# A decoder layer on one core: the output projection with tokens on the output's partitions, and expert loads of 2 MB from the fifth expert on

## Chip, core and metric

One core of one Trainium2 chip runs the whole program. The metric is the device time of one execution in microseconds (us). Engines: TensorE (PE in the rows, PEld its weight loads), VectorE (DVE), ScalarE (ACT), GpSimd (POOL) and SyncE (SP), whose queue issues nearly all loads from HBM.

## The reference, cut

The layer takes h (256 tokens by 1024 features) in float32. Sub-layer 1 mixes tokens by two branches (sparse attention and RWKV-7), gates and merges them and projects the result; sub-layer 2 sends each token to 2 of 32 experts of one group of eight.

```python
merged = jax.nn.sigmoid(gate_a) * (o_attn @ w_branch_attn[l]) + jax.nn.sigmoid(gate_r) * (o_rwkv @ w_branch_rwkv[l])
h = h + gt1 * (merged @ w_out[l])                 # w_out: 1024 x 1024
xn2 = _rmsnorm(h, moe_norm_g[l]) * (1.0 + sc2) + sh2
# routing: group = argmax of 4 group logits, then the top 2 of its 8 experts
hdn = jax.nn.silu(xt @ wg) * (xt @ wu)            # wg, wu: 1024 x 512, for each of 32 experts
acc + cw[:, None] * (hdn @ wd)                    # wd: 512 x 1024
h = h + gt2 * moe
```

## The kernel before

*Front.* Projections, RWKV, attention and gates are generators of work pieces, and the string ORDER says which generator goes next. LORD sorts the loads of weights, RESERVE keeps room for each stage. Float32 precision comes from `mm3` (L539 to 541): both operands are split in a high and a low part, and three matmuls stand for one. `split` (L526 to 529) makes the parts of a weight: a cast on ScalarE or GpSimd, a subtraction on VectorE or GpSimd, chosen by the two letters of SPLIT's entry for the stage. The last two pieces of the front are the branch projections "br" and "ba"; their merged output lies split in `xhi` and `xlo`, features on partitions.

*Output projection* (L1462 to 1527, "wo"). Eight blocks m of output features are on the partitions of PSUM and all 256 tokens in the columns. Weights come in four loads j of two k each (k: blocks of 128 input features). `out_part` takes the weights of block m at a stride, so that block m holds the features 8p+m:

```python
mm3(block(m), (w[0][:, m:1024:8], w[1][:, m:1024:8]), (mh[:, k, :], ml[:, k, :]), k == 0 and m > 5,
    k == 7 and m not in (0, 2, 4))
```

These are 8 m x 8 k x 3 = 192 matmuls. x was transposed into `h` (features on partitions) during the front (L1072). The residual is added by VectorE (L1519), squares and router logits follow by small matmuls (`squares`, L1485; `logits`, L1479), and `turn` (L1491) transposes h into `h2`, tokens on partitions.

*Routing* (L1562 to 1613) stands on VectorE for both halves of the tokens at once: the root of the mean square (L1562 to 1571), logits and top choices (L1578 to 1593). TensorE then makes the ranks (L1597), `places` one-hot tables, `begin` (L1714) copies h2 into the accumulators, and `fetch` (L1624) gathers the tokens of each expert: matmuls whose weights are h2 and whose moving operand is a one-hot table.

*Experts.* Four experts make a quad, eight quads in all; a quad's products are `row_in` and `rows_in` (L1645, L1639) for gate and up, L1666 for down. Each expert has 6 MB, the whole 201 MB. SyncE issues their loads in a fixed order (`pump`, L296), each into the first slot that is free: in the main arena, or in the two pools `sb1` and `sb2` that take the place of the split buffers after their last use. Quads 0 and 1 come in loads of 1 MB (quad 0's first gate in four row pieces of each expert), later ones in 2 MB (WHOLE = 2), the last quad's down weights in halves of 512 columns. The next quad's places, fetch and scatter stand between a quad's up and down products.

## Time and profile before

| | |
|---|---|
| device time, median of 3 runs | 801.64 us (800.87 to 804.71) |
| the profiled execution | 800.6 us, span 798.8 us |
| TensorE busy | 660.6 us, 83% of the span |
| VectorE, ScalarE, GpSimd busy | 277.0, 164.9, 132.9 us |
| moved by DMA | 261.36 MB, 327 GB/s in the mean |
| chain that ended last | DMA 33%, TensorE 27%, VectorE 1% of the span |

Times in the rows are microseconds from the start of the span. TensorE's granted clock is given as a share of full speed: 1.00 is 2.4 GHz, 0.50 is 1.2 GHz. Matmuls are pipelined, so a matmul's duration is longer than the distance from one start to the next; the distance is what a row of them costs.

### The profile page before, as it was taken

How to read it: one execution, taken by the hardware profiler on the slowest of the kernel's cores; microseconds unless marked ns; L12 is line 12 of the kernel's file. 1: busy time of each engine (PE TensorE's matmuls, PEld its weight loads, DVE VectorE, ACT ScalarE, POOL GpSimd, SP SyncE). 2: the span in 40 equal slices, each digit the busy share in tenths (PEclk: the TensorE clock that was granted, in tenths of full speed). 3: DMA queues.
4: the chain of work that ended last, by engine and by line, in shares of the span. 5: the costliest groups of instructions: out<-in, count | busy, mean ns of one | idle time of the engine just before them, and what ended most of it. 6: DMA issues, size and time to landing. Idle time of an engine off the chain costs nothing.

```text
span 798.8 us, 11321 instructions
## 1 busy us (share of the span) xinstructions
PE 660.6 (83%) x4657; PEld 379.2 (47%) x4657; DVE 277.0 (35%) x665; ACT 164.9 (21%) x350; POOL 132.9 (17%) x171
## 2 busy tenths in 40 slices
PE   5898988899999999989998586777676777778567
PEld 2785657568889889974442131131131132222112
DVE  2577799887255645141211061011010010010001
ACT  2445412343176631031110010010010010000000
POOL 1456643322235133220000000000000000000000
PEclk9899999999999999989999698889889899889879
DMA  9997476552758368249999999999999999999995
GB/s 334 392 309 245 143 261 241 175 192 81 244 191 284 106 235 344 66 162 377 422 420 428 427 425 431 425 427 432 425 428 429 427 427 428 427 428 427 427 394 201
DMA packets 53796, 261.36 MB, mean 327 GB/s; under 512 B 6864, under 2 KB 18128, under 8 KB 37360
## 3 DMA queue, kind: packets, MB, share of 16 engines
q1 hardware_dynamic: 53456, 260.11, 82.4%
q8 instruction: 37, 0.61, 0.3%
q10 hardware_dynamic: 288, 0.52, 0.2%
q14 instruction: 15, 0.12, 0.0%
HBM read 259.57 MB, written 1.05 MB: 326 GB/s over the span
## 4 chain that ended last, share of the span: by engine, by line
DMA 33%; PE 27%; DVE 1%; SPq 1%; POOL 1%; ACT 0%; issue 0%; ACTq 0%; POOLq 0%
DMA more<-in_expert_w_up_dram 12%; DMA more<-in_expert_w_down_dram 11%; DMA more<-in_expert_w_gate_dram 10%; PE ps_e L1639 10%; PE ps_e L1666 4%; PE ps_e L1624 2%; PE ps_a L541 1%; PE ps_a L539 1%; PE ps_a L540 1%; PE acc L1721 1%; PE ps_e L1673 1%; PE acc L1714 1%; SPq L296 1%; PE ps_r L539 0%; PE ps_r L540 0%; PE ps_r L541 0%
## 5 line engine op out<-in xcount | busy, mean ns | idle before, releaser
L1639 PE MATMUL ps_e<-arena,more 128*32 128x512 f32 x456 | 83.9, 693 | 24.2 <-DMA arena<-in_expert_w_gate_dram 18.3
L1639 PE MATMUL ps_e<-arena 128*32 128x512 f32 x424 | 81.9, 709 | 22.4 <-DMA arena<-in_expert_w_up_dram 12.4
L1666 PE MATMUL ps_e<-arena 128*32 128x512 f32 x360 | 73.5, 659 | 17.6 <-DMA arena<-in_expert_w_down_dram 12.9
L529 DVE TENSOR_TENSOR split<-arena,split 128x512 fp32r<-128x512 f32 x77 | 61.3, 805 | 57.7 <-POOL split L526 29.1
L528 ACT CAST split<-arena 128x512 fp32r<-128x512 f32 x71 | 43.3, 618 | 74.6 <-PE ps_g L540 29.3
L573 PE MATMUL ps_a<-split 128*128 128x256 f32 x360 | 52.1, 303 | 3.3 <-ACT split L484 1.9
L1650 ACT ACTIVATE arena<-ps_e 128x512 f32<-128x512 f32 x8 | 4.8, 597 | 239.2 <-PE ps_e L1639 239.2
L1651 DVE SCALAR_TENSOR_TENSOR arena<-arena,ps_e 128x512 f32<-128x512 f32 x8 | 5.5, 688 | 140.0 <-ACT arena L1650 140.0
L573 PEld LDWEIGHTS ps_a<-split 128*128 128x128 f32 x360 | 47.8, 204 | 12.6 <-issue 6.8
L529 POOL TENSOR_TENSOR split<-arena,split 128x512 fp32r<-128x512 f32 x33 | 45.3, 1372 | 48.6 <-ACT split L528 25.5
L1704 POOL TENSOR_TENSOR arena<-arena 128x256 f32<-128x256 f32 x8 | 4.9, 616 | 283.4 <-PE ps_e L1707 281.8
L1683 DVE TENSOR_TENSOR arena<-ps_e,more 128x512 f32<-128x512 f32 (+1 forms) x17 | 11.8, 692 | 112.9 <-PE ps_e L1666 103.7
L1639 PEld LDWEIGHTS ps_e<-arena,more 128*32 128x32 f32 x456 | 18.6, 126 | 60.8 <-issue 27.7
L1639 PEld LDWEIGHTS ps_e<-arena 128*32 128x32 f32 x424 | 18.2, 128 | 56.4 <-issue 26.1
L1666 PE MATMUL ps_e<-more,arena 128*32 128x512 f32 x88 | 34.9, 632 | 8.4 <-DMA more<-in_expert_w_down_dram 7.7
L526 POOL TENSOR_SCALAR split<-arena 128x512 fp32r<-128x512 f32 x39 | 26.8, 688 | 82.9 <-PE ps_r L540 23.8
L1639 PE MATMUL ps_e<-more,arena 128*32 128x512 f32 x56 | 31.3, 722 | 10.7 <-DMA more<-in_expert_w_gate_dram 10.7
L1666 PEld LDWEIGHTS ps_e<-arena 128*32 128x32 f32 x360 | 16.5, 117 | 49.0 <-issue 22.5
L1639 PE MATMUL ps_e<-more,more 128*32 128x512 f32 x56 | 30.3, 702 | 10.6 <-DMA more<-in_expert_w_up_dram 10.6
L1652 DVE SCALAR_TENSOR_TENSOR arena<-arena,ps_e 128x512 f32<-128x512 f32 x8 | 8.2, 1029 | 87.3 <-PE ps_e L1639 87.3
L539 PE MATMUL ps_g<-split 128*128 128x256 f32 x128 | 38.3, 299 | 0.0
L1624 PEld LDWEIGHTS ps_e<-arena,more 128*128 128x128 f32 x256 | 30.9, 196 | 12.9 <-issue 8.2
(379 smaller groups left out, 1263.0 us busy)
## 6 DMA issues: line engine op xcount, KB each, us to landing
arena<-in_expert_w_gate_dram SPq DMA_DIRECT2D x21, 2048.0 KB, 22.3
arena<-in_expert_w_up_dram SPq DMA_DIRECT2D x21, 2048.0 KB, 23.6
arena<-in_expert_w_down_dram SPq DMA_DIRECT2D x17, 2048.0 KB, 21.1
arena<-in_w_in_dram SPq DMA_DIRECT2D x18, 1024.0 KB, 8.1
arena<-in_expert_w_down_dram SPq DMA_DIRECT2D x18, 1024.0 KB, 17.9
arena<-in_ada_w_dram SPq DMA_DIRECT2D x16, 1024.0 KB, 6.8
arena<-in_expert_w_up_dram SPq DMA_DIRECT2D x14, 1024.0 KB, 9.8
arena<-in_expert_w_gate_dram SPq DMA_DIRECT2D x12, 1024.0 KB, 8.3
```

What stands on the lines that cost most here:

```text
L296: nc.sync.dma_start(out=dst, in_=src)
L526: nc.gpsimd.tensor_scalar(h, w, 1.0, 0.0, op0=OP.mult, op1=OP.add)
L528: nc.scalar.copy(h, w)
L529: (nc.gpsimd if p[1] == "P" else nc.vector).tensor_sub(l, w, h.bitcast(F32))
L539: nc.tensor.matmul(ps, l[0], r[0], start=start, stop=False)
L540: nc.tensor.matmul(ps, l[0], r[1], start=False, stop=False)
L573: nc.tensor.matmul(p, a[:, kk, :], b[:, 4 * hf + kk, :], start=(i == 0 and kk == KORD[0]), stop=(i == 2 and kk == KORD[-1]))
L1624: nc.tensor.matmul(ps[:, n * kk:n * kk + n], h2[:, a, 2 * k2 + kk, :], oh(a), start=(a == 0), stop=(a == 1))
L1639: nc.tensor.matmul(ps[32 * g:32 * g + 32, :], xg[:, k, 32 * g:32 * g + 32], w[:, k - 4 * i, :], start=(k == 0), stop=(k == 7))
L1652: nc.vector.scalar_tensor_tensor(hidb[0:r].rearrange("p (j q) -> p q j", j=4), thb[0:r].rearrange("p (q j) -> p q j", j=4), 0.5, psu[0:r, ...
L1666: nc.tensor.matmul(pss[c][32 * g:32 * g + 32, :], hTb[:, j, 32 * g:32 * g + 32], w[:, j - 2 * i, 512 * c:512 * c + 512], start=(j == 0), s ...
L1683: nc.vector.tensor_mul(Yb[0:r, c:c + 512], ps[0:r], gt2[0][0:r, g:g + 512])
```

## The change

The output projection has four blocks (a, c) in PSUM: half a of the tokens on the partitions, 512 output features c in the columns. The weights of its matmuls are now the split activations `xhi` and `xlo` (128 tokens, contiguous), the moving operand is 512 contiguous columns of w_out: 4 blocks x 8 k x 3 = 96 matmuls. The residual stream `h2` has tokens on partitions and features in natural order from the start; the transposes of x in the front, the zero matmuls ahead of the projection and the copies to h2 are gone, and `fetch` reads h2 as weights at a stride of 8. gt1 is spread over all partitions by `mod_bcast` (two matmuls). Squares are summed by ScalarE's accumulator, the transposes that the logits need are four matmuls for each block, and root and routing are done for each half of the tokens. The string LAST sets the order of the last k pair: O is a block's product, T its transposes, L its logits, N the root, R the routing.

`xhi` and `xlo` of the first four k lie in a pool of their own, so that `sb1` (now 4096 columns) is opened after the second weight load and `sb2` (6144) after the last block. Loads are 2 MB from quad 1 on (WHOLE = 1), and the last quad's up weights are halves too. `begin` goes block by block, two ahead of the row products and two between them; the weights of the routing (`weights`) are worked out after quad 0's first products; quad 1's preparation stands behind quad 0's down products. ORDER and LORD are other strings (not shown).

```diff
-RESERVE = (29696, 17408, 24576, 4096, 0)
+RESERVE = (25600, 17408, 20480, 4096, 0)
...
-SPLIT = (('PD', 'PD', 'AP', 'AD'), ('PD', 'PD', 'AP', 'AD'), ('PP', 'PP', 'AD', 'AD'), ('AD', 'AP', 'AD', 'AD'), ('AD', 'PD', 'AP', 'PD'))
+SPLIT = (('PD', 'PD', 'AP', 'AD'), ('PD', 'PD', 'AD', 'AD'), ('AP', 'PP', 'AP', 'AD'), ('AD', 'AP', 'AP', 'AD'), ('AD', 'PD', 'AP', 'PD'))
...
-WHOLE = 2
+WHOLE = 1
+BEGIN = 1
+LAST = 'O00 O01 O10 O11 O20 O21 T00 O30 T01 L00 O31 L01 N0 R0 T10 T11 N1 L10 L11'
...
-    B = Arena(fr.__enter__().tile([128, nB], F32R, name="split"), nB)
+    B = Arena(fr.__enter__().tile([128, nB - 2048], F32R, name="split"), nB - 2048)
+    fr1 = tc.tile_pool(name="fr1", bufs=1, side="right")
+    B1 = Arena(fr1.__enter__().tile([128, 2048], F32R, name="split1"), 2048)
...
-        return q >= WHOLE and not (n == "ed" and q == QUADS - 1)
+        return q >= WHOLE and not (n != "eg" and q == QUADS - 1)
...
-    nc.sync.dma_start(out=wrt[:, :, 0:4], in_=I["router_group_w"][0].rearrange("(p k) n -> p k n", p=128))
-    nc.sync.dma_start(out=wrt[:, :, 4:36], in_=I["router_expert_w"][0].rearrange("(p k) n -> p k n", p=128))
+    nc.sync.dma_start(out=wrt[:, :, 0:4], in_=I["router_group_w"][0].rearrange("(k p) n -> p k n", p=128))
+    nc.sync.dma_start(out=wrt[:, :, 4:36], in_=I["router_expert_w"][0].rearrange("(k p) n -> p k n", p=128))
...
-    xhi = B.get(8, T)
-    xlo = B.get(8, T)
+
+    xhl = [b.get(4, 2, T) for b in (B1, B)]
+
+    def xhi(k, s=slice(0, T)):
+        return xhl[k // 4][:, k % 4, 0, s]
+
+    def xlo(k, s=slice(0, T)):
+        return xhl[k // 4][:, k % 4, 1, s]
...
-        h = M(8, T)
...
+        h2 = M(2, D)
...
-        xt = M(2, D)
-        nc.sync.dma_start(out=xt, in_=I["x"][0].rearrange("(a p) d -> p a d", p=128))
...
+        nc.sync.dma_start(out=h2, in_=I["x"][0].rearrange("(a p) d -> p a d", p=128))
...
-        for q in range(4):
-            ps = PS()
-            for kk in range(2):
-                for a in range(2):
-                    nc.tensor.transpose(ps[:, kk * 256 + a * 128:kk * 256 + a * 128 + 128],
-                                        xt[:, a, 2 * q + kk:D:8], ident)
-            nc.scalar.copy(h[:, 2 * q:2 * q + 2, :], ps.rearrange(v2, a=2))
-            yield 0.5
-        A.free(xt)
...
-            gt1, sh2 = mod_cols(row1, (0, 2))
-            nc.vector.tensor_scalar(gt1, gt1, 0.5, None, op0=OP.mult)
+            gt1 = M(1024)
+            mod_bcast(gt1, row1, 0, 0.5)
+            sh2, = mod_cols(row1, (2,))
...
-    fr2.__exit__(None, None, None)
-    state["more"].append(Arena(pool(name="sb1", bufs=1, side="right").tile([128, nB2], F32, name="more0"), nB2))
...
-    psl = PS("r")
-    pso = [PS(t) for t in "aaarr"]
-
-    for ps in pso[0:3] + [psl]:
-        nc.tensor.matmul(ps, zero.bitcast(BF16), trib[:, None, 128:256].to_broadcast([128, 4, 128]), start=True, stop=False)
...
-    def logits(m):
...
-            nc.tensor.matmul(psl[:, 64 * a:64 * a + 36], h[:, m, 128 * a:128 * a + 128], wrt[:, m, :],
...
-    def turn(m):
-
-        pst = PS("g")
-        for a in range(2):
-            nc.tensor.transpose(pst[:, 128 * a:128 * a + 128], h[:, m, 128 * a:128 * a + 128], ident)
-        nc.scalar.copy(h2[:, :, m, :], pst[:, 0:256].rearrange("p (a c) -> p a c", a=2))
-
-    def block(m):
-        return pso[m // 2][:, 256 * (m % 2):256 * (m % 2) + 256] if m < 6 else pso[m - 3][:, 0:256]
-
-    def out_part(m, k, w):
-        mm3(block(m), (w[0][:, m:1024:8], w[1][:, m:1024:8]), (mh[:, k, :], ml[:, k, :]), k == 0 and m > 5,
-            k == 7 and m not in (0, 2, 4))
+    pso = [PS(t) for t in "aaar"]
+    psl = [PS("r"), PS("r")]
+    tb = [M(512), M(512)]
+    st = M(4)
+    hts = [hx[:, 512 * i:512 * i + 512].rearrange("p (k t) -> p k t", k=4) for i in range(2)]
...
+    def leave_room(name, cols, *before, **k):
+        for p in before:
+            p.__exit__(None, None, None)
+        state["more"].append(Arena(pool(name=name, bufs=1, **k).tile([128, cols], F32, name="more" + name), cols))
+        pump()
+
+    def out_part(a, c, k, w):
+        s = slice(128 * a, 128 * a + 128)
+        mm3(pso[2 * a + c], (xhi(k, s), xlo(k, s)), (w[0][:, 512 * c:512 * c + 512], w[1][:, 512 * c:512 * c + 512]), k == 0,
+            k == 7)
+
+    def residual(a, c):
+
+        hv = h2[:, a, 512 * c:512 * c + 512]
+        for o in (0, 256) if a and c else (0,):
+            r = slice(o, o + 256 if a and c else 512)
+            nc.vector.tensor_mul(tb[c][:, r], pso[2 * a + c][:, r], gt1[:, 512 * c:512 * c + 512][:, r])
+            (nc.vector if a else nc.gpsimd).tensor_add(hv[:, r], hv[:, r], tb[c][:, r])
+        nc.scalar.activation(tb[c], hv, AF.Square, scale=1.0 / 32, accum_out=st[:, 2 * c + a:2 * c + a + 1])
+
+    def turn(a, c):
+
+        ps = PS("g")
+        for kk in range(4):
+            nc.tensor.transpose(ps[:, 128 * kk:128 * kk + 128], h2[:, a, 512 * c + 128 * kk:512 * c + 128 * kk + 128], ident)
+        nc.scalar.copy(hts[c], ps.rearrange("p (k t) -> p k t", k=4))
+
+    def logits(a, c):
+
+        for kk in range(4):
+            k = 4 * c + kk
+            nc.tensor.matmul(psl[a][:, 0:36], hts[c][:, kk, :], wrt[:, k, :], start=(k == 0), stop=(k == 7))
...
-            if j < 3:
-                for m in range(8):
-                    out_part(m, 2 * j + kk, ws[kk])
-                continue
-            for m in range(8 if kk else 0):
-                for k2 in range(2):
-                    out_part(m, 6 + k2, ws[k2])
-                for n in {3: (0,), 4: (1,), 5: (2,), 6: (3,), 7: (4, 5)}.get(m, ()):
-                    logits(n)
...
-                    nc.vector.scalar_tensor_tensor(h[:, n, :], block(n), gt1[:, n:n + 1], h[:, n, :], op0=OP.mult, op1=OP.add)
...
-        done(("wo", j))
-
-    fr.__exit__(None, None, None)
-    state["more"].append(Arena(pool(name="sb2", bufs=1).tile([128, nB], F32, name="more"), nB))
-    h2 = state["more"][-1].get(2048, from_top=False).rearrange("p (a k c) -> p a k c", a=2, k=8)
-    turn(0)
-    turn(1)
-    logits(6)
-    turn(2)
...
-    squares()
-    for m in range(3, 8):
-        turn(m)
-    A.free(h)
-    A.free(gt1)
+            if kk:
+                done(("wo", j))
+            for n in range(4 if j < 3 else 0):
+                out_part(n // 2, n % 2, 2 * j + kk, ws[kk])
+        if j == 1:
+            leave_room("sb1", nB2 + 2048, fr2, fr1, side="right")
+    last[0] = None
+
+    def out_last(n, kk):
+        after_last(lambda: out_part(n // 2, n % 2, 6 + kk, ws[kk]))
+        if kk:
+            residual(n // 2, n % 2)
...
+    def root(a):
+
+        z, y, u = zz[:, :, a:a + 1], y8[:, a:a + 1], u8[:, a:a + 1]
+        nc.vector.scalar_tensor_tensor(z[:, 0], st[:, a:a + 1], 1e-6, st[:, 2 + a:3 + a], op0=OP.add, op1=OP.add)
+        nc.vector.tensor_scalar(y.bitcast(I32), z[:, 0].bitcast(I32), -0.5, float(0x5F3759DF), op0=OP.mult, op1=OP.add)
+        for r in range(1, 3):
+            nc.vector.tensor_scalar(z[:, r], z[:, 0], 0.25 ** r, None, op0=OP.mult)
+        for r in range(3):
+            nc.vector.scalar_tensor_tensor(u, y, y, z[:, r], op0=OP.mult, op1=OP.mult)
+            nc.vector.scalar_tensor_tensor(y, u, -3.0, y, op0=OP.add, op1=OP.mult)
+        nc.vector.tensor_scalar(rs2[:, a:a + 1], y, -0.125, None, op0=OP.mult)
...
+    def route(a):
...
+        nc.vector.tensor_scalar(selb[:, a], eq[:, a], -2.0e38, None, op0=OP.is_lt)
+
+
+    for what in LAST.split():
+        f, i = what[0], [int(c) for c in what[1:]]
+        if f == "O":
+            out_last(*i)
+        elif f in "TL":
+            after_last(lambda: (turn if f == "T" else logits)(*i))
+            if f == "L" and i[1]:
+                nc.scalar.copy(lg[:, i[0]], psl[i[0]][:, 0:36])
+        elif f == "N":
+            root(*i)
+        else:
+            route(*i)
+    leave_room("sb2", nB - 2048, fr)
...
+    acc = [acp.tile([128, 512], F32, name=f"acc{i}") for i in range(4)]
+
+    def begin(n):
+
+        nc.tensor.matmul(acc[n], ident, h2[:, n // 2, 512 * (n % 2):512 * (n % 2) + 512], start=True, stop=False)
+
+    for n in range(BEGIN):
+        after_last(lambda: begin(n))
+    route(1)
...
+            nc.tensor.matmul(psk[:, 32 * a:32 * a + 32], trib[:, 0:128], selb[:, a], start=True, stop=(a == 0))
+        nc.tensor.matmul(psk[:, 32:64], trib[:, 128:256], selb[:, 0], start=False, stop=True)
+
+    after_last(ranks)
+    for n in range(BEGIN, 2):
+        after_last(lambda: begin(n))
+    nc.vector.tensor_mul(rk, psk[:, 0:64].rearrange("p (a n) -> p a n", a=2), selb)
+
+    def weights():
+
+        nc.gpsimd.tensor_copy(sel, selb)
...
-                    nc.tensor.matmul(ps[:, n * kk:n * kk + n], h2[:, a, 2 * k2 + kk, :], oh(a), start=(a == 0),
+                    nc.tensor.matmul(ps[:, n * kk:n * kk + n], h2[:, a, 2 * k2 + kk:D:8], oh(a), start=(a == 0),
...
-    def begin():
-
-        for a in range(2):
-            for c in range(2):
-                nc.tensor.matmul(acc[2 * a + c].rearrange("p (c k) -> p c k", k=8), ident,
-                                 h2[:, a, :, 64 * c:64 * c + 64].rearrange("p k c -> p c k"), start=True, stop=False)
...
-                        fetch(0, [k2])
-                        for k in () if i else (2 * k2, 2 * k2 + 1):
-                            row_in(ps, XGb[0], need(("row", k)), k)
-                            done(("row", k))
+                        after_last(lambda: fetch(0, [k2]))
+                    for k in range(0 if i else 4):
+                        after_last(lambda: row_in(ps, XGb[0], need(("row", k)), k))
+                        done(("row", k))
+                        if k % 2:
+                            after_last(lambda: begin(2 + k // 2))
                     if i == 0:
                         continue
-                rows_in(ps, XGb[q % 2], [need((n, e, i)) for e in es], i)
+                    weights()
+                after_last(lambda: rows_in(ps, XGb[q % 2], [need((n, e, i)) for e in es], i), q == 0)
...
-            begin()
...
-        places(q + 1)
-        fetch(q + 1)
-        scatter(q + 1)
+
+        def prepare():
+            places(q + 1)
+            fetch(q + 1)
+            scatter(q + 1)
+
+        if q:
+            prepare()
...
+        if q == 0:
+            prepare()
```

TensorE from the last block to the ranks or accumulators. L539 to L541 (L550 to L552 after) are the projection's matmuls, L1479 and L1505 logits, L1491 and L1498 transposes, L1485 squares, L1597 ranks, L1592 `begin`. Before:

```order
L539 MATMUL ps_r<-split 128x256
L540 MATMUL ps_r<-split 128x256
L541 MATMUL ps_r<-split 128x256
L1479 MATMUL ps_r<-arena 128x36 x4
L1491 MATMUL ps_g<-arena 128x128 x4
L1479 MATMUL ps_r<-arena 128x36 x4
L1491 MATMUL ps_g<-arena 128x128 x2
L1485 MATMUL ps_r<-arena 128x1 x6
L1491 MATMUL ps_g<-arena 128x128 x10
L1597 LDWEIGHTS arena
L1597 MATMUL ps_g<-arena 128x32
L1597 LDWEIGHTS arena
```

After:

```order
L550 MATMUL ps_r<-split 128x512
L551 MATMUL ps_r<-split 128x512
L552 MATMUL ps_r<-split 128x512
L1498 MATMUL ps_g<-arena 128x128 x4
L1505 MATMUL ps_r<-arena 128x36 x4
L550 MATMUL ps_r<-split 128x512
L551 MATMUL ps_r<-split 128x512
L552 MATMUL ps_r<-split 128x512
L1505 MATMUL ps_r<-arena 128x36 x4
L1498 MATMUL ps_g<-arena 128x128 x8
L1505 MATMUL ps_r<-arena 128x36 x8
L1592 MATMUL acc_3227<-arena 128x512
```

Transposes and logits of half 0 now stand around the last matmuls, those of half 1 behind them; the squares are gone from TensorE.

VectorE from the last residual on. L1519, L1522 (L1490, L1491 after) are residuals and a square, L1562 to L1571 (L1544 to L1551) the root, L1578 to L1593 (L1555 to L1565) the routing. Before:

```order
L1519 SCALAR_TENSOR_TENSOR arena<-ps_r,arena 128x256 x2
L1522 TENSOR_TENSOR arena<-arena 128x256
L1562 TENSOR_SCALAR arena<-ps_r 128x2
L1563 TENSOR_SCALAR arena<-arena 128x2
L1565 TENSOR_SCALAR arena<-arena 128x2 x2
L1568 SCALAR_TENSOR_TENSOR arena<-arena 128x1 x2
L1571 SCALAR_TENSOR_TENSOR arena<-arena 128x1 x2
L1568 SCALAR_TENSOR_TENSOR arena<-arena 128x1 x2
L1571 SCALAR_TENSOR_TENSOR arena<-arena 128x1 x2
L1568 SCALAR_TENSOR_TENSOR arena<-arena 128x1 x2
L1571 SCALAR_TENSOR_TENSOR arena<-arena 128x1 x2
L1578 SCALAR_TENSOR_TENSOR arena<-ps_r,arena 128x36 x2
```

After, from half 1's last residual on:

```order
L1490 TENSOR_TENSOR arena<-ps_r,arena 128x256 x2
L1491 TENSOR_TENSOR arena<-arena 128x256 x2
L1551 TENSOR_SCALAR arena<-arena 128x1
L1555 SCALAR_TENSOR_TENSOR arena<-arena 128x36
L1557 TENSOR_REDUCE arena<-arena 128x1
L1558 MATCH_REPLACE arena<-arena 128x8
L1561 SCALAR_TENSOR_TENSOR arena<-arena 128x32
L1544 SCALAR_TENSOR_TENSOR arena<-arena 128x1
L1562 MAX arena<-arena 128x8
L1545 TENSOR_SCALAR arena<-arena 128x1
L1547 TENSOR_SCALAR arena<-arena 128x1
L1563 COPY arena<-arena 128x2
```

The root of half 0 now stands ahead of these rows; its routing and half 1's root alternate.

SyncE's loads at the turn from quad 0 to quad 1: `arena`, `more` and `moresb` are where a load goes, 128x2048 is 1 MB, 128x4096 2 MB. Before:

```order
L296 DMA arena<-in_expert_w_down_dram 128x2048 x2
L296 DMA more<-in_expert_w_down_dram 128x2048
L296 DMA arena<-in_expert_w_down_dram 128x2048
L296 DMA more<-in_expert_w_down_dram 128x2048 x2
L296 DMA arena<-in_expert_w_down_dram 128x2048 x2
L296 DMA arena<-in_expert_w_gate_dram 128x2048 x8
L296 DMA arena<-in_expert_w_up_dram 128x2048 x7
L296 DMA more<-in_expert_w_up_dram 128x2048
L296 DMA more<-in_expert_w_down_dram 128x2048 x2
```

After:

```order
L300 DMA moresb_3057<-in_expert_w_up_dram 128x2048
L300 DMA moresb_3057<-in_expert_w_down_dram 128x2048
L300 DMA arena<-in_expert_w_down_dram 128x2048 x2
L300 DMA moresb_3216<-in_expert_w_down_dram 128x2048 x3
L300 DMA arena<-in_expert_w_down_dram 128x2048 x2
L300 DMA arena<-in_expert_w_gate_dram 128x4096 x4
L300 DMA arena<-in_expert_w_up_dram 128x4096
L300 DMA moresb_3057<-in_expert_w_up_dram 128x4096
L300 DMA arena<-in_expert_w_up_dram 128x4096
L300 DMA moresb_3216<-in_expert_w_up_dram 128x4096
```

Three of quad 0's last six loads go to the second pool, and quad 1 begins with loads of 2 MB.

## Rows read from the trace of the kernel before

**Rows 1.** Slices of the page: GB/s that DMA moved, 40 slices of 20 us.

```profile
GB/s 334 392 309 245 143 261 241 175 192 81 244 191 284 106 235 344 66 162 377 422 420 428 427 425 431 425 427 432 425 428 429 427 427 428 427 428 427 427 394 201
```

**Rows 2.** Windows, TensorE: stretch, length, busy (instructions), granted clock, DMA share, GB/s.

```profile
0.00:300.30 300.30, 272.79 (x2477) 0.97 0.66 229
...
306.00:337.00 31.00, 31.00 (x131) 1.00 0.48 177
...
356.70:363.00 6.30, 5.80 (x19) 0.57 0.99 416
```

**Rows 3.** Timeline, SyncE's loads: start, duration, queue, line, operation, destination and source, count.

```profile
325.78 11.87 SPq L296 DMA_DIRECT2D arena<-in_expert_w_down_dram  x2
348.85 0.33 SPq L296 DMA_DIRECT2D more<-in_expert_w_down_dram  x1
...
367.64 7.36 SPq L296 DMA_DIRECT2D arena<-in_expert_w_gate_dram  x6
```

**Rows 4.** Timeline, TensorE, projection's end to experts; [idle before, its releaser].

```profile
348.42 0.40 PE L541 MATMUL ps_r<-split 128*128 128x256 f32 x1
348.66 0.98 PE L1479 MATMUL ps_r<-arena 128*128 128x36 f32 x8
...
356.67 0.23 PE L1597 MATMUL ps_g<-arena 128*128 128x32 bf16 x2 [2.18 <-DVE arena L1593]
...
357.43 2.05 PE L1714 MATMUL acc<-more,arena 128*128 128x512 f32 x2 [0.50 <-DVE arena L1608]
359.30 1.89 PE L1624 MATMUL ps_e<-arena,more 128*128 128x128 f32 x8
...
362.82 1.50 PE L1645 MATMUL ps_e<-arena 128*32 128x512 f32 x12
```

**Rows 5.** Timeline, TensorE: branch projections, then the output projection's first matmul.

```profile
299.64 0.28 PE L539 MATMUL ps_g<-split,split 128*128 128x256 f32 x1
299.76 0.28 PE L540 MATMUL ps_g<-split,split 128*128 128x256 f32 x1
...
300.30 0.51 PE L539 MATMUL ps_a<-split 128*128 128x256 f32 x1
```

**Rows 6.** Timeline, TensorE: query projection.

```profile
162.24 0.40 PE L541 MATMUL ps_a<-split 128*128 128x512 f32 x1
162.48 0.39 PE L539 MATMUL ps_a<-split 128*128 128x512 f32 x1
```

**Rows 7.** Timeline, splits of weights in the output projection.

```profile
317.99 0.62 ACT L528 CAST split<-arena 128x512 fp32r<-128x512 f32 x1 [5.14 <-PE ps_r L540]
317.99 0.62 POOL L526 TENSOR_SCALAR split<-arena 128x512 fp32r<-128x512 f32 x1 [5.15 <-PE ps_r L540]
...
318.64 0.69 DVE L529 TENSOR_TENSOR split<-arena,split 128x512 fp32r<-128x512 f32 x1 [4.47 <-POOL split L526]
318.69 1.78 POOL L529 TENSOR_TENSOR split<-arena,split 128x512 fp32r<-128x512 f32 x1
```

**Rows 8.** Timeline, VectorE: a residual, start of root, start of routing.

```profile
348.86 0.48 DVE L1519 SCALAR_TENSOR_TENSOR arena<-ps_r,arena 128x256 f32<-128x256 f32 x1 [1.41 <-PE ps_r L541]
...
352.44 0.16 DVE L1562 TENSOR_SCALAR arena<-ps_r 128x2 f32<-128x2 f32 x1 [2.56 <-PE ps_r L1485]
...
354.22 0.41 DVE L1578 SCALAR_TENSOR_TENSOR arena<-ps_r,arena 128x36 f32<-128x36 f32 x2
```

**Rows 9.** Windows, all engines: PE, PEld, DVE, ACT, POOL; clock, DMA, GB/s.

```profile
370.00:380.00 10.00, 10.00 (x96) 2.86 (x88) 0.69 (x1) 1.16 (x3) 0.00 (x0) 1.00 1.00 407
...
400.00:420.00 20.00, 20.00 (x140) 8.53 (x136) 3.02 (x8) 2.47 (x6) 0.62 (x1) 1.00 1.01 421
500.00:600.00 100.00, 71.78 (x408) 23.57 (x406) 9.81 (x21) 5.53 (x13) 1.23 (x2) 0.86 1.01 428
```

**Rows 10.** Timeline, TensorE: a fetch, and quad 1's first expert matmuls.

```profile
385.52 3.73 PE L1624 MATMUL ps_e<-arena,more 128*128 128x128 f32 x32
...
397.80 7.89 PE L1639 MATMUL ps_e<-arena,more 128*32 128x512 f32 x66
```

More of the change, by code (lines that the diff above doesn't have):

```diff
@@ new lines, in layer_kernel @@
+    for what in LAST.split():
[11 more added lines that the diff above has]
+    leave_room("sb2", nB - 2048, fr)
+    A.free(gt1, *tb)
+    pump()
+    pctx.__exit__(None, None, None)
```

158 lines of the change are left out of this document (58 added, 100 removed).

## The prediction

> **What bounds the kernel now.** I read the page's slices first (20 us each, counted from 0): from slice 19 to the last but two DMA moves 420 to 432 GB/s, in slice 16 it moves 66 and in 17 it moves 162 [rows 1]. So the second half is a stream of expert weights (32 x 6 MB = 201 MB) at a constant rate, and the end is the time at which this stream gets going, plus bytes by rate. In the first half TensorE is the busy engine: 272.8 of the first 300.3 us [rows 2]. Between the two the stream starves, because SBUF is full and slots are freed only by the output projection, the routing and the first experts. SyncE's timeline shows that: two loads from 325.8, one at 348.9, the first loads of quad 1 from 367.6 [rows 3]. The reader is to see what each of them follows on TensorE: 348.9 the last projection matmul of 348.42, 367.6 the first expert products from 362.82 [rows 4]. An earlier start of the experts is therefore worth its full length, as long as the stream doesn't run dry later.
>
> **The projection.** Call s the start of its first matmul, 300.30 [rows 5]. Before: 192 matmuls of 256 columns, the last from 348.42 to the logits' start at 348.66 [rows 4]: 48.4 us, 0.25 a matmul, 0.24 the last. The same shape (128x128 weights, 256 columns) starts every 0.12 us in the branch projections just ahead [rows 5]. It is not the clock: in 306 to 337 the granted clock is 1.00 [rows 2], the 2.4 GHz level. The one difference in the code is that the weights are read at a stride of 8 elements. After: 96 matmuls of 512 columns with 128 contiguous columns as weights; that form stands in the query projection and starts every 0.24 us [rows 6]. 96 x 0.24 = 23.0. Among the last blocks now stand 8 transposes and 4 matmuls for logits. Eight 128x128 fp32 matmuls took 1.89 us in 359.3 to 361.2 [rows 4], where the clock was 0.57 [rows 2]; at the full level I take half, 0.9. Four logit matmuls are half of 0.98 [rows 4], 0.5. The logits wait for ScalarE's copy of the transposes, which stands behind squares: 1.0, somewhat more than one 512-column operation there (0.62 [rows 7]); and 0.2 for the last k's start. The last projection matmul ends at s+25.6, where it was s+48.4: 22.8 less.
>
> **Splits.** Each k needs two splits, a cast (0.62 on ScalarE or GpSimd) and a subtraction (0.69 on VectorE, 1.78 on GpSimd [rows 7]). A k now lasts 12 x 0.24 = 2.9 on TensorE instead of 5.8 or more. By SPLIT's last row ('AD', 'PD', 'AP', 'PD') two k cost GpSimd two casts and a subtraction, 2 x 0.62 + 1.78 = 3.0, VectorE 3 x 0.69 = 2.1, ScalarE 1.2, against 5.8 on TensorE. If the engines run side by side that is enough, and I cost it at nothing; as one chain, 0.62 + 1.78 + 0.62 + 0.69 = 3.7, it would not be (rival 1).
>
> **From the last projection matmul to the first expert.** Before, 14.2 us: logits, squares and turns until VectorE's root at 352.44, the routing of both halves from 354.22, ranks at 356.67, two pairs of matmuls that start the accumulators (the first pair 2.05) with fetch between, experts at 362.82 [rows 4, 8]. After, half 0's residual, squares and root lie beside the last blocks, and its routing stands between the steps of half 1's root on VectorE. Half 1 keeps its residual in two pieces of 256 columns, four operations of 0.48 [rows 8], 1.9; the square and two handovers, 0.9 (0.62 as above and 0.3); the root, 1.7 (352.44 to 354.22 is 1.8 for both halves [rows 8], and one half has the same chain of dependent steps); the routing, 1.8 (354.22 to 356.67 is 2.4 for both). Half 1's turn and logits hide beside the root. That is s+31.9. Then ranks, product and places, 1.8 (ranks to fetch was 2.6 [rows 4], with an accumulator pair ahead of the fetch), and fetch with its copies 2.5. Fetch has got slower work: it takes h2 in natural order as weights, at a stride of 8 elements, as the old projection did. I price its 8 matmuls like those, 8 x 0.24 = 1.9 (contiguous they took 1.89 at the low clock [rows 4] and 3.73 for 32, 0.12 each, at the full one [rows 10]), and 0.6 for copies. First expert matmul at s+36.2, bounds 35.3 (the stride costs fetch nothing) and 38 (all at 1.2 GHz, where the strided fetch may take 3.7). The gain is 62.5 - 36.2 = **26.3**, 22.8 of it in the projection, the rest in the gap of 10.6 after 14.2.
>
> **What is late next: the stream.** Call the first expert matmul R before and R' after. Before, quad 1's first load is issued at R+4.8 [rows 3, 4], with some of quad 0 still queued, whose last I put at R+8 (two loads of 1 MB, 2.5 us each at 421 GB/s [rows 9], ahead of it). After, by the order of the loads, three of quad 0's are let go by the last projection matmul and two by the first row products; the latter two land at about R'+7.8 by the same count. The first 2 MB load follows the last of the row products; the second follows the first half of the gate, a hole that I put at 0.5. Net +0.3.
>
> **2 MB loads.** In quad 1 the 1 MB loads ran at 407 and 421 GB/s, the 2 MB loads later at 428 [rows 9]: 25 MB, 62 us at 407 and 59 at 428, a gain between 0 and 3 (62 - 59); the 407 holds for 10 us only, so I take 0.5 (10 us by 5% of 407 against 428). The price is that a slot of 2 MB comes free later. Eight such loads last 8 x 4.9 = 39 us, so the stream runs dry at R'+47 unless a ninth is issued. The ninth waits until quad 1's gate has been read. Before, quad 1's first matmul is at 397.80, R+35.0, and half of that group's 7.89 us [rows 10] makes it R+39. After, TensorE has more to do until there: quad 1's fetch, 32 matmuls at 0.24 instead of 0.12, 3.9; the rest of quad 0's fetch, half as much, 1.9; against that one of the two accumulator pairs now lies ahead of R', 2.0 less. R'+43: a cover of 4 us. In later quads fetch's 3.9 is hidden, as TensorE is busy for 72 of 100 us in 500 to 600 [rows 9]; without that cover it would be 3.9 for each of some six quads, 23.
>
> **Ahead of the projection.** Gone are 16 transposes, 2 x 0.9 = 1.9, and four zero matmuls of 512 columns, 4 x 0.24 = 1.0. New are two fp32 matmuls that spread gt1 over the partitions, between 1.0 and 2.05 (a pair took 2.05 near the low level [rows 4]); I take 1.9. Net -1.0. The planner's tables (ORDER, LORD, SPLIT, RESERVE) are new too and rearrange 300 us in which TensorE idles 27.5 [rows 2]; no row prices that. I take 0, with -4 and +4 as bounds, a seventh of that idle time either way. The tail does the same work; its loads in halves: 0.
>
> **Sum.** -26.3 + 0.3 - 0.5 - 1.0 = -27.5. The profiled execution took 800.6, which gives 773.1; it lies 1.0 under the median of 801.64, by which it is 774.1. I say **773.5**.
>
> **Rivals.**
> 1. *Splits bound the projection.* If each k pays the whole chain, 3.7 and 0.4 of handovers instead of 2.9, six k add 7: 780. For: GpSimd's 1.78 alone is more than half of a k's 2.9 [rows 7]. Against: two pairs of buffers, and 3.0 of 5.8 on the busiest engine. 0.08.
> 2. *The queue runs dry between quads 0 and 1.* It decides from 4 us of lateness of quad 1's gate beyond my count, which a strided fp32 fetch at 0.36 or more a matmul would bring; a hole of 3 to 8 gives 777 to 781. For: preparing quad 1 now stands behind quad 0's down products, with the slower fetch. Against: the count. 0.09.
> 3. *The front's new order gives back* what the removed work saves, with 4 to 6 us of new waits: 779. For: 27.5 us of idle time that hang on the order. 0.04.
> 4. *Matmul time follows columns, however weights lie.* The projection then keeps its 48 us (192 x 256 columns are 96 x 512), and only the gap's 3.6 and the 1.2 of the other terms remain: 796. Against: 0.12 and 0.24 for one shape at one clock [rows 2, 4, 5]. 0.02. The Trainium skill has this rule ("TensorE: Matmul & The Clock Gate", section "Back-to-back issue gap"): 262 cycles for 256 columns, 518 for 512, and no term for the layout of the weights. The branch rows agree with it, the old projection's rows do not.
> 5. *Slower than before: TensorE stays at the 1.2 GHz level through quads 0 and 1*, because the gap breaks up its work, as at 356.7 to 363.0, where 0.57 was granted [rows 2]. Each quad could then take up to its 35 us more; the queue empties from 4 us of lateness, each further one is one at the end, and from 4 + 28 = 32 on the kernel is slower than before: 802 to 812. Against: clock 1.00 from 370 on [rows 9]. 0.03.
>
> **How the numbers follow.** Forecast 0.74, rivals 0.26. The forecast's own range is -4 and +4 for the front, -0.9 and +1.8 for the gap, -0.5 and +0.5 for the rate: 768 to 780. To hold 8 in 10 it takes in rivals 1 to 3 above, and below the whole 3 of the rate: **765 to 782**. Faster by over 0.5% (about what a measurement of this kernel can tell from no change; below 797.6) are the forecast and rivals 1 to 3: 0.74 + 0.08 + 0.09 + 0.04 = 0.95. Rival 4 lies at that border, and its 0.02 is the chance of within 0.5%; rival 5 is slower, 0.03.
>
> **What would show it.** In the trace after: projection matmuls of 512 columns 0.23 to 0.24 apart, without idle time put down to VectorE or GpSimd; the last one ending 25 to 26 us behind the start of the first; the first expert matmul at 36; DMA's share at 1.0 from 8 us behind that until the tail, with no hole between quads 0 and 1; the first projection matmul at 299 to 300. Wrong would be: a first projection matmul off by more than 4, a spacing above 0.3, a low granted clock beyond the first experts, or a second hole in DMA.

## The result: 778.4 us, ratio 0.9705, and the profile after

The changed kernel takes 778.38 us (median of 4 runs, 777.42 to 781.20) against 802.2 before; the ratio is 0.9705, 95% interval 0.9669 to 0.9741. The forecast was 773.5 in a range of 765 to 782: the direction, most of the size and the range held, the time that came is that of rival 2. The profiled execution took 777.42 us, span 775.6. First the page's slices again:

```profile
GB/s 332 386 307 237 166 281 249 208 171 82 268 249 191 109 218 261 414 300 392 379 414 428 429 424 431 429 423 430 427 426 430 427 428 427 427 431 425 421 394 205
```

Slices are 19.4 us long here. The two starved slices 16 and 17 of before [rows 1] carry 414 and 300 GB/s now. But slice 19 (368 to 388) shows 379, where before every slice from 19 on, up to the tail, had 420 or more. TensorE's timeline, from the projection to the first experts (start, duration, line; a wait in brackets), in the places of [rows 4, 5]:

```profile
295.75 0.39 PE L550 MATMUL ps_a<-split,split 128*128 128x512 f32 x1
295.98 0.39 PE L551 MATMUL ps_a<-split,split 128*128 128x512 f32 x1
...
301.58 0.50 PE L551 MATMUL ps_a<-split,split 128*128 128x512 f32 x1 [1.32 <-DVE split L540]
...
321.82 1.08 PE L1505 MATMUL ps_r<-arena 128*128 128x36 f32 x8 [0.57 <-ACT arena L1499]
...
323.52 0.98 PE L1505 MATMUL ps_r<-arena 128*128 128x36 f32 x8
...
332.03 3.87 PE L1645 MATMUL ps_e<-arena 128*128 128x128 f32 x16
335.83 1.92 PE L1666 MATMUL ps_e<-arena 128*32 128x512 f32 x16
```

The projection runs from 295.75 to 323.52, 27.8 us for 48.4; its matmuls of 512 columns are 0.23 apart. The first expert matmul stands at 335.83, 27.0 earlier than before. The span got only 23.2 shorter, so 3.8 were lost behind it. Windows from the first expert matmul to the end, of before and of after (length, TensorE busy, granted clock, DMA share, GB/s):

```profile
362.82:798.80 435.98, 328.42 (x1915) 0.88 0.98 413
```

```profile
335.83:775.60 439.77, 350.68 (x1907) 0.91 0.97 408
```

The clock is not lower; the same bytes (180 and 179 MB) move at 408 instead of 413 GB/s. Windows of 2 us show where:

```profile
336.00:338.00 2.00, 2.00 (x17) 1.00 0.01 4
348.00:350.00 2.00, 2.00 (x24) 1.00 0.29 115
350.00:352.00 2.00, 2.00 (x24) 1.00 1.00 262
...
384.00:386.00 2.00, 2.00 (x22) 1.00 0.54 229
386.00:388.00 2.00, 2.00 (x13) 1.00 0.70 123
388.00:390.00 2.00, 2.00 (x10) 1.00 0.77 319
```

The last three are a hole that before did not have: against 428 GB/s they lack 2.9 us of transfer. A smaller hole, 2.2 us in 348 to 352, stands while quad 0's gate is read; the prediction had put 0.5 on it. SyncE's loads and TensorE's work say what the larger one waits for:

```profile
340.80 12.42 SPq L300 DMA_DIRECT2D arena<-in_expert_w_gate_dram  x4
355.87 0.33 SPq L300 DMA_DIRECT2D arena<-in_expert_w_up_dram  x1
362.74 0.33 SPq L300 DMA_DIRECT2D moresb<-in_expert_w_up_dram  x1
363.16 0.38 SPq L300 DMA_DIRECT2D arena<-in_expert_w_up_dram  x1
366.18 0.33 SPq L300 DMA_DIRECT2D moresb<-in_expert_w_up_dram  x1
386.18 1.88 SPq L300 DMA_DIRECT2D arena<-in_expert_w_down_dram  x4
```

```profile
366.10 7.88 PE L1645 MATMUL ps_e<-arena 128*128 128x128 f32 x32
373.82 0.38 PE L1723 MATMUL ps_e<-arena 128*128 128x128 f32 x2
374.13 1.05 PE L1660 MATMUL ps_e<-arena 128*32 128x512 f32 x4
375.11 1.98 PE L1730 MATMUL acc<-arena 128*128 128x512 f32 x4
377.03 1.04 PE L1660 MATMUL ps_e<-arena 128*32 128x512 f32 x2
378.00 1.98 PE L1730 MATMUL acc<-arena 128*128 128x512 f32 x4
379.92 7.06 PE L1660 MATMUL ps_e<-arena 128*32 128x512 f32 x60
```

Eight loads of 2 MB are issued from 340.80 to 366.18 and then none for 20 us. The next four wait until quad 1's gate has been read (L1660, until about 386). Ahead of it on TensorE: a fetch of 7.88 us (3.73 before, [rows 10]), and, in the middle of the gate's first products, quad 0's accumulation (L1730), 4.0 us.

### The profile page after: what moved, and what is told of

The parts are those of the page before. It is cut to its first block, busy times and chain, and to the rows that moved or that the text cites. A ratio compares the mean times of both kernels' runs of the same rounds, so it can differ in the third digit from the quotient of the medians.

```text
span 775.6 us, 11041 instructions
## 1 busy us (share of the span) xinstructions
PE 658.5 (85%) x4531; PEld 376.5 (49%) x4531; DVE 272.7 (35%) x662; ACT 166.6 (21%) x351; POOL 136.9 (18%) x169
## 4 chain that ended last, share of the span: by engine, by line
DMA 39%; PE 36%; DVE 10%; POOL 5%; issue 4%; SPq 3%; ACT 2%; POOLq 0%; DVEq 0%; ACTq 0%
DMA arena<-in_expert_w_gate_dram 13%; DMA arena<-in_expert_w_down_dram 12%; PE ps_e L1660 9%; DMA arena<-in_expert_w_up_dram 8%; DMA moresb<-in_expert_w_up_dram 4%; PE ps_a L584 3%; PE ps_g L550 3%; PE ps_e L1645 3%; PE ps_g L551 3%; PE ps_e L1687 3%; PE ps_g L552 3%; SPq L300 3%; POOL arena L595 1%; DMA arena<-in_ada_w_dram 1%; DVE split L540 1%
## 5 line engine op out<-in xcount | busy, mean ns | idle before, releaser
L1660 PE MATMUL ps_e<-arena 128*32 128x512 f32 x752 | 146.6, 652 | 26.9 <-DMA arena<-in_expert_w_gate_dram 24.4
L1687 PE MATMUL ps_e<-arena 128*32 128x512 f32 x352 | 80.3, 703 | 24.5 <-DMA arena<-in_expert_w_down_dram 20.2
L1660 PE MATMUL ps_e<-moresb,arena 128*32 128x512 f32 x240 | 82.5, 648 | 11.4 <-DMA moresb<-in_expert_w_gate_dram 7.6
L1660 PEld LDWEIGHTS ps_e<-arena 128*32 128x32 f32 x752 | 34.0, 119 | 98.7 <-issue 57.8
L1645 PEld LDWEIGHTS ps_e<-arena 128*128 128x128 f32 x256 | 62.3, 334 | 12.3 <-issue 7.1
L1645 PE MATMUL ps_e<-arena 128*128 128x128 f32 x256 | 64.5, 407 | 0.0
L539 ACT CAST split<-arena 128x512 fp32r<-128x512 f32 x75 | 45.9, 618 | 54.0 <-PE ps_g L551 25.8
L1704 DVE TENSOR_TENSOR arena<-ps_e,arena 128x512 f32<-128x512 f32 (+1 forms) x17 | 11.7, 691 | 129.9 <-PE ps_e L1687 115.3
L1687 PEld LDWEIGHTS ps_e<-arena 128*32 128x32 f32 x352 | 19.1, 124 | 76.1 <-issue 37.4
L1687 PE MATMUL ps_e<-moresb,arena 128*32 128x512 f32 x96 | 48.8, 740 | 5.1 <-DMA moresb<-in_expert_w_down_dram 4.4
L1660 PEld LDWEIGHTS ps_e<-moresb,arena 128*32 128x32 f32 x240 | 18.8, 118 | 42.3 <-issue 24.7
L550 PE MATMUL ps_g<-split,split 128*128 128x256 f32 x128 | 37.5, 293 | 0.0
L551 PE MATMUL ps_g<-split,split 128*128 128x256 f32 x128 | 36.2, 283 | 0.0
L552 PE MATMUL ps_g<-split,split 128*128 128x256 f32 x128 | 36.1, 282 | 0.0
L1730 PE MATMUL acc<-arena 128*128 128x512 f32 (+1 forms) x68 | 31.9, 607 | 0.8 <-DVE arena L1704 0.8
L1650 ACT ACTIVATE arena<-ps_e,arena 128x128 f32<-128x128 f32 x32 | 12.9, 454 | 74.0 <-PE ps_e L1645 74.0
## 6 DMA issues: line engine op xcount, KB each, us to landing
arena<-in_expert_w_gate_dram SPq DMA_DIRECT2D x22, 2048.0 KB, 27.5
```

The costliest lines, as they stand in the source:

```text
L539: nc.scalar.copy(h, w)
L550: nc.tensor.matmul(ps, l[0], r[0], start=start, stop=False)
L551: nc.tensor.matmul(ps, l[0], r[1], start=False, stop=False)
L552: nc.tensor.matmul(ps, l[1], r[0], start=False, stop=stop)
L1645: nc.tensor.matmul(ps[:, n * kk:n * kk + n], h2[:, a, 2 * k2 + kk:D:8], oh(a), start=(a == 0), stop=(a == 1))
L1660: nc.tensor.matmul(ps[32 * g:32 * g + 32, :], xg[:, k, 32 * g:32 * g + 32], w[:, k - 4 * i, :], start=(k == 0), stop=(k == 7))
```

## Experiments

All times are medians beside runs of the kernel before on the same chip; ratios are against those, and the changed kernel's 0.9705 is what they are compared with.

**Quad 0's accumulation behind quad 1's products.** The other half of the change stays.

```diff
-                finish(stb[(q - 1) % 2], c)
+                if q == 1:
+                    after_last(lambda: finish(stb[(q - 1) % 2], c))
+                else:
+                    finish(stb[(q - 1) % 2], c)
```

> The changed kernel, with quad 0's accumulation (four matmuls of 512 columns, 4.0 us on TensorE in the trace after) tied behind quad 1's up products instead of standing among the first matmuls of quad 1's gate. Theory A (the end is set by the hole in DMA at 384 to 390 us, which ends when quad 1's gate has been read through at 386.18): the gate's slots come free 4.0 us earlier, the hole's 2.9 us of lost transfer go, 775.5 us. Theory B (the hole is only the echo of the start of the stream, or is made up later): no change, 778.4 us. Theory C (what stands behind the up products then delays their slots instead): 778 to 782 us.

Measured: 775.32 us, ratio 0.9675 (0.9661 to 0.9689). The loads that were issued at 386.18 now go at 381.65, and the hole is gone:

```profile
381.65 1.75 SPq L300 DMA_DIRECT2D arena<-in_expert_w_down_dram  x4
```

```profile
384.00:386.00 2.00, 2.00 (x10) 1.00 1.00 426
386.00:388.00 2.00, 2.00 (x11) 1.00 0.96 410
388.00:390.00 2.00, 2.00 (x7) 1.00 1.02 434
```

Theory A: releasing those slots 4.5 us earlier gives back about the hole's 2.9 and no more (3.1 us by the medians, 2.4 by the ratios). The two ratios' intervals overlap by a little, and the windows carry the verdict.

**Quad 1 in loads of 1 MB.** `WHOLE = 2` in the changed kernel.

> The changed kernel with quad 1's loads of 1 MB again (2 MB from quad 2 on). Theory A (the hole comes from the grain of quad 1's slots): the first slots of quad 1's gate come free when half of it is read, some 4 to 7 us earlier; the hole's 2.9 us go, and 25 MB at 407 to 421 instead of 428 GB/s cost 0.9 to 3: 776.4 to 778.5 us. Theory B (2 MB loads are a gain, the hole has another cause): 779.3 to 781.5 us.

Measured: 775.95 us, ratio 0.9688 (0.9672 to 0.9704). In the same windows 426, 414 and 426 GB/s move: the finer slots close the hole too, with the accumulation still in the gate. As a time the difference from the changed kernel is not proved (0.9688 and 0.9705 overlap); it is on theory A's side. What 2 MB loads gain in rate is small: windows of the changed kernel and of this one,

```profile
352.00:384.00 32.00, 31.27 (x198) 1.00 1.00 428
```

```profile
352.00:384.00 32.00, 31.27 (x199) 1.00 1.01 422
```

For quad 1's 25 MB that is an estimate of 0.8 us, less than the hole.

**2 MB loads alone.** `WHOLE = 1` in the kernel before.

> The kernel before with 2 MB loads from quad 1 on, and nothing else. Theory A (cover is enough there, since its fetch is contiguous and no accumulation stands in the gate): 25 MB at 428 instead of 407 to 421 GB/s, 0.5 to 1.5 us less: 800.7 to 801.7 us against 802.2. Theory B (slots of 2 MB come free too late there as well): a hole of 2 to 5 us, 804 to 807 us.

Measured: 806.56 us, ratio 1.0067 (1.0052 to 1.0082), slower, as theory B had it, but not in the place that I meant. Windows of this kernel:

```profile
370.00:372.00 2.00, 2.00 (x20) 1.00 0.71 295
372.00:374.00 2.00, 2.00 (x24) 1.00 0.09 37
374.00:376.00 2.00, 2.00 (x24) 1.00 0.66 131
...
410.00:412.00 2.00, 2.00 (x19) 1.00 0.91 254
```

```profile
373.94 4.29 SPq L296 DMA_DIRECT2D arena<-in_expert_w_gate_dram  x4
```

3.8 us of transfer are missing where quad 1's first 2 MB load waits, until 373.94, for TensorE's products of quad 0's gate (L1639); before, the first load of 1 MB goes at 367.64 [rows 3]. 0.8 are missing at the end of quad 1's gate; in before the same windows show 422, 430, 406 and 426. So this part of the change by itself is a loss of 5 us in the old kernel, and in the new one no gain is left.

**The stride of the weights, in the old projection.** The output is no longer the reference's: the blocks hold other features, and everything behind them computes with those.

```diff
-        mm3(block(m), (w[0][:, m:1024:8], w[1][:, m:1024:8]), (mh[:, k, :], ml[:, k, :]), k == 0 and m > 5,
+        mm3(block(m), (w[0][:, 128 * m:128 * m + 128], w[1][:, 128 * m:128 * m + 128]), (mh[:, k, :], ml[:, k, :]), k == 0 and m > 5,
```

> The kernel before with 128 contiguous columns of w_out as the weights of each block, instead of 128 columns at a stride of 8; the blocks then hold other features, so it times the projection and computes something else. Theory A (the stride of the weight read is what the 0.24 us are): the 192 matmuls start 0.12 us apart, 48.4 becomes 24 to 28 (then splits wait), and the first expert matmul comes 20 to 24 us earlier: 778 to 782 us unless tokens are routed so differently that work is added at the end. Theory B (time goes by columns, or the splits hold the old projection too): 0.24 stays, 801 us.

A single run, 778.09 us (801.47 before). TensorE's timeline:

```profile
299.98 0.28 PE L539 MATMUL ps_a<-split 128*128 128x256 f32 x1
300.10 0.28 PE L540 MATMUL ps_a<-split 128*128 128x256 f32 x1
...
340.08 1.92 PE L1645 MATMUL ps_e<-arena 128*32 128x512 f32 x16
```

192 matmuls of 256 columns, 0.12 apart; the first expert matmul comes 22.7 earlier. Theory A: the 0.24 were the stride of the weight read and nothing else. TensorE's weight loads show it directly, before and in this run:

```profile
317.13 0.34 PEld L539 LDWEIGHTS ps_r<-split 128*128 128x128 f32 x1
```

```profile
317.04 0.19 PEld L539 LDWEIGHTS ps_a<-split 128*128 128x128 f32 x1
```

Where the change moved tokens to the output's partitions, what paid was that this brought contiguous weights: the old layout with contiguous weights reaches the changed kernel's time. That is one run, with other features in the router, so the first expert matmul says more here than the whole time. Here the Trainium skill's page "TensorE: Matmul & The Clock Gate", section "Back-to-back issue gap", holds for contiguous weights (262 cycles for 256 columns, an estimate of 0.11 us at 2.4 GHz, 0.12 measured), and 0.24 for the strided ones is a case that it doesn't have.

**The stride of the weights, in the new fetch.** Again the output is not the reference's, since the experts get other features.

```diff
-                    nc.tensor.matmul(ps[:, n * kk:n * kk + n], h2[:, a, 2 * k2 + kk:D:8], oh(a), start=(a == 0),
+                    nc.tensor.matmul(ps[:, n * kk:n * kk + n], h2[:, a, 128 * (2 * k2 + kk):128 * (2 * k2 + kk) + 128], oh(a), start=(a == 0),
```

> The changed kernel with fetch reading 128 contiguous columns of h2 as weights instead of columns at a stride of 8; the experts then get other features in their rows, so it times the fetch and computes something else. Theory A (a strided weight read costs about 0.12 us for each 128 columns, as in the old projection): fetch's matmuls start 0.12 us apart instead of 0.24, the first expert matmul comes 1.9 us earlier, quad 1's gate 7.7 us earlier; the hole at 384 to 390 goes, and the whole stream stands 2 to 4 us earlier: 771.5 to 773.6 us. Theory B (the stride costs float32 fetches nothing, their 0.24 us have another cause): no change, 778.4 us.

Measured: 773.37 us, ratio 0.9655 (0.9640 to 0.9669), on theory A's side.

```profile
331.76 2.05 PE L1645 MATMUL ps_e<-arena 128*128 128x128 f32 x16 [0.24 <-DVE arena L1713]
333.83 1.93 PE L1666 MATMUL ps_e<-arena 128*32 128x512 f32 x16
...
362.20 3.84 PE L1645 MATMUL ps_e<-arena 128*128 128x128 f32 x32
```

Sixteen records take 2.05 instead of 3.87, and quad 1's 32 take 3.84 instead of 7.88. It is not the clock: that 7.88 stands in windows with 1.00 granted. The change cured the strided read in the projection and put one into fetch, which costs 4 us of the whole time (0.0050 of 801; the two intervals touch at 0.9669).

**The planner's tables.** ORDER, LORD, SPLIT and RESERVE of the kernel before in the changed one, and the other way round.

> The changed kernel with ORDER, LORD, SPLIT and RESERVE of the kernel before. In the trace after the first projection matmul stands at 295.75 us, 4.55 earlier than before; the prediction gave 1.0 of it to removed work and left the tables at 0, -4 to +4. Theory A (the tables bring the other 3.5): it stands at 298.5 to 300, and the time is 2.5 to 4.5 over the changed kernel's 778.4: 781 to 783 us. Theory B (the removed transposes and VectorE's order at the last branch bring all): 295 to 297, 777.5 to 779.5 us.

> The kernel before with ORDER, LORD, SPLIT and RESERVE of the changed one. Theory A (these tables are worth some 3.5 us ahead of the projection wherever they stand): its first matmul at 296 to 297.5 instead of 300.3, 798 to 799.5 us against 801.4. Theory B (they fit only the changed code, or carry nothing): 300 to 303, 801 to 804 us.

Measured: 783.02 us, ratio 0.9753 (0.9708 to 0.9798), and 796.36 us, ratio 0.9930 (0.9908 to 0.9952). The projection's first matmul, in the changed kernel with old tables and in the old kernel with new ones:

```profile
301.42 0.40 PE L550 MATMUL ps_a<-split,split 128*128 128x512 f32 x1
```

```profile
295.29 0.51 PE L539 MATMUL ps_a<-split 128*128 128x256 f32 x1
```

The start goes with the tables, whichever code stands behind: over all traces here it lies at 295.3 to 297.7 with the new and at 300.0 to 301.4 with the old. They are worth about 5 us of the time (4.6 in the changed kernel, 5.1 in the old one); the removed transposes and zero matmuls show nothing of their own above this scatter of some 2 us.

**Products first, routing behind.** LAST in plain order, so that half 0's transposes, logits and root come after all products.

```diff
-LAST = 'O00 O01 O10 O11 O20 O21 T00 O30 T01 L00 O31 L01 N0 R0 T10 T11 N1 L10 L11'
+LAST = 'O00 O01 O10 O11 O20 O21 O30 O31 T00 L00 T01 L01 T10 L10 T11 L11 N0 R0 N1'
```

> The changed kernel with LAST in plain order: all products of the last two k first, then transposes and logits of both halves, then root and routing. Theory A (laying half 0's routing beside the last blocks takes work off the path): the last projection matmul comes some 2 us earlier, at 25.5 to 26 behind the first, the first expert matmul 1 to 3 us later than 335.8; 779.4 to 781.4 us. Theory B (VectorE's chain for half 1 sets the end of the gap either way, and the interleaving only delays the last block): the first expert matmul 0 to 2 us earlier, 776.4 to 778.4 us.

Measured: 784.81 us, ratio 0.9779 (0.9739 to 0.9819): theory A, and twice the upper end of its price.

```profile
325.32 1.74 PE L1505 MATMUL ps_r<-arena 128*128 128x36 f32 x8 [1.95 <-ACT arena L1499]
...
345.59 1.92 PE L1666 MATMUL ps_e<-arena 128*32 128x512 f32 x16
```

```profile
326.00:340.00 14.00, 11.59 (x47) 0.50 0.66 273
```

The last product ends 25.1 behind the first (27.8 in the changed kernel), yet the first expert matmul comes 22.8 behind it instead of 12.3. Transposes and logits run one after the other, each group of logits waiting for ScalarE's copy, and from 326 to 340 TensorE is granted 0.50, the 1.2 GHz level; the changed kernel has 0.88 in the same window, in which it is already at other work. So the interleaving is worth 6 us; how much of that is the lower clock and how much the waits, no run separates. The front began 1.9 later in this trace than in the other one (297.69 and 295.75); it lies that far apart in other traces with the same tables as well (297.44 in the first of the four versions below), so I don't count it as an effect of LAST.

**Four versions on top.** The first has the accumulation moved (as above) and the last two `begin` blocks behind quad 0's up products; the second is the first with `WHOLE = 2`; the third is the first with the splits ('AD', 'AD', 'AP', 'AD') in the projection; the fourth is the third with a second copy of h2 in fetch's order, made by ScalarE beside the routing (with all four `begin` blocks ahead of the fetch and the natural h2 freed for a load).

> The changed kernel with quad 0's accumulation behind quad 1's up products (as in a_finish) and the last two blocks of begin behind quad 0's up products instead of between its row products. In the trace of a_finish the last hole in DMA is at 348 to 352 us, 2.2 us of lost transfer, and ends when quad 0's gate has been read through. Theory A (each such hole is set by TensorE's work up to the release that ends it): two fp32 blocks of 512 columns, 1.0 us each, leave that path, the hole shrinks to 0.3: 773.4 us. Theory B (the hole ends by something else, the landing of the loads themselves): as a_finish, 775.3 us.

> As best1, but with quad 1 in loads of 1 MB (2 MB from quad 2 on). Theory A (with the accumulation out of the gate the 2 MB slots are released early enough, and only the rate of the loads differs): 0.3 to 1.0 us over best1: 773.7 to 774.4. Theory B (the finer grain still closes holes): 0.5 to 1.5 under best1, 771.9 to 772.9 us.

> As best1, with the projection's splits by ('AD', 'AD', 'AP', 'AD') instead of ('AD', 'PD', 'AP', 'PD'): three casts of four on ScalarE. In the trace after TensorE waits 0.22, 1.32 and 0.36 us for VectorE's subtractions at the start of the projection, where GpSimd's casts take 1.06 and ScalarE is idle for 3 us. Theory A (the late casts on GpSimd are what these waits come from): 1.2 to 1.9 us less than best1, 771.5 to 772.2 us. Theory B (VectorE's own work for the last branch is the bound there): as best1, 773.4 us, or 0.5 more since ScalarE's casts collide with squares at the end.

> As best3, with a second copy of h2 in the order that fetch wants (four copies of 128x512 on ScalarE, some 0.6 us each, beside the routing; 2048 columns of the second pool), so that fetch reads contiguous weights and still gathers the right features; all four begin matmuls stand ahead of the fetch, and the slots of the natural h2 are given to a load behind them. Theory A (the strided fetch is what is left on TensorE's path, 3.87 us for 16 matmuls against 2.05 contiguous): the first row products come 0 to 1 us earlier (1.8 less for fetch, 1 to 2 more for two begins), quad 0's gate is read through 2.7 to 3.7 earlier, quad 1's 6 to 7 earlier, and the holes at 348 to 352 and 382 to 386 (1.6 us of lost transfer in best3) close: 771.5 to 773 us against best3's 773.7. Theory B (the stream is held by the first release at 336.5, which the two begins ahead of it delay as much as fetch gains): 773.5 to 775 us.

Measured: 775.36 us (ratio 0.9671, 0.9648 to 0.9693), 777.66 (0.9675, 0.9649 to 0.9700), 773.68 (0.9652, 0.9630 to 0.9674) and 773.88 (0.9652, 0.9626 to 0.9678). The first two are where the accumulation alone was: the two `begin` blocks show no gain (theory B by the time; the hole at 350 to 354 did shrink to 0.8, but in that trace the projection began 1.3 later, so this is not settled). In the third the wait of 1.32 on VectorE that I aimed at is still there, with 1.70, so theory A's reason does not hold for it, and the 1.5 us under the first version lie within the intervals. In the fourth the mechanism came as told:

```profile
333.64 1.95 PE L1654 MATMUL ps_e<-arena,moresb 128*128 128x128 f32 x16
335.52 3.64 PE L1675 MATMUL ps_e<-arena 128*32 128x512 f32 x32
```

```profile
348.00:350.00 2.00, 2.00 (x24) 1.00 0.97 401
350.00:352.00 2.00, 2.00 (x19) 1.00 1.03 434
```

Fetch is contiguous, and no hole is left behind 340; but the first row products are where they were, since two `begin` blocks now stand ahead of them (39.5 behind the projection's start, 39.4 in the third version), and the median is the same (771.8 to 776.1). Theory B by the time. All four are faster than the kernel before; against the changed kernel (0.9669 to 0.9741) each interval still overlaps by a little, and among the four the runs don't decide.

## Why the prediction came near, and which step was wrong

| step | predicted | measured |
|---|---|---|
| start of the projection | -1.0 | -4.6 |
| length of the projection | -22.8 | -20.6 |
| gap to the first expert | -3.6 | -1.9 |
| first expert matmul, sum of these | -27.3 | -27.0 |
| stream behind it | -0.2 | +3.8 |
| span | -27.5 | -23.2 |

*The bound and the projection* were read rightly. The strided weight read was named from two rows for one shape at one clock, and undoing it alone brings the first expert matmul 22.7 earlier, what was claimed for the projection. Of the 2.2 that are missing, 1.9 are three waits for VectorE in the first k's (0.22, 1.32, 0.36), a mild form of rival 1. VectorE's and GpSimd's rows there:

```profile
296.44 2.38 DVE L540 TENSOR_TENSOR split<-arena,split 128x512 fp32r<-128x512 f32 x2
```

```profile
298.24 1.06 POOL L537 TENSOR_SCALAR split<-arena 128x512 fp32r<-128x512 f32 x1
...
303.79 0.62 POOL L537 TENSOR_SCALAR split<-arena 128x512 fp32r<-128x512 f32 x1 [1.79 <-PE ps_r L552]
```

I took 0.69 and 0.62 from a place where both engines have time [rows 7]; at the end of the last branch, where both are busy, two subtractions take 2.38 and a cast 1.06. Before, the same lengths were covered by 5.8 us of TensorE for each k. Both engines being at work is not the whole reason: the cast of 303.79 takes 0.62 beside VectorE's subtractions, and in [rows 7] VectorE takes 0.69 beside GpSimd's 1.78. That VectorE's work for the last branch is what the waits come from is argued; the third version shows only that moving casts off GpSimd leaves the longest of them.

*The gap* was mis-sized in the term of fetch. I counted 8 matmuls ahead of the first row products; the source has two fetch pieces there, and each of their float32 matmuls leaves two records: 16 records, 3.87 us, for my 1.9. With the projection's 2.2 this puts the first expert matmul at s+40.1, outside the bounds of 35.3 to 38.

*The step that failed* is in the part on 2 MB loads: "The ninth waits until quad 1's gate has been read. Before, quad 1's first matmul is at 397.80, R+35.0, and half of that group's 7.89 us makes it R+39." The group of 66 records is not gate and up, of which half is the gate: the gate has 4 x 8 = 32 matmuls, 64 records, and is the whole group. Read through is R+42.9 before. That is 3.9, and 4.0 more come from the accumulation, which the order of TensorE's instructions put among the gate's first products; it stood behind the gate before, and I had looked past that piece of the order. R'+43 becomes R'+51; 386.18 is R'+50.4 (the rest of quad 0's fetch, put at 1.9 more, takes 0.6 more, 3.85 for 3.21), and the stream ran dry some 49 behind R', where I had 47. With the right count the cover of 4 us is a lack of 4 (47 against 51), and rival 2, at 0.09, would have been the forecast: its 777 to 781 hold the 778.4. It came by the count, not by the slow fetch that rival 2 names: fetch's records are 0.25 apart, as forecast. A smaller term of the same part, the wait for the second 2 MB load, was put at 0.5 and lacks 2.2.

*2 MB loads* were put at a gain of 0.5 with an open price. Alone they cost 5 in the old kernel, and going back to 1 MB in quad 1 of the new one doesn't make it slower: the sign of the whole was wrong. The 407 GB/s of 370 to 380 were mostly not the size of the loads (1 MB loads move 422 in 352 to 384), and the later release costs more than the rate gives.

*The front* was put at 0 with -4 to +4 for the tables, for want of a row. They gave 5, by both exchanges. That the first expert matmul came within 0.3 of the sum is therefore luck, and no proof of its parts: 3.6 more from the front cover 2.2 less in the projection and 1.7 less in the gap.

*Rivals 3 to 5* did not come: the front gained, the old projection's 256 columns go at 0.12 once their weights are contiguous, and the granted clock is 1.00 in the windows of 334 to 390.
